# Down projections of a two-block kernel: T sums made ahead by POOL and kept in DRAM, bank sums added to the residual by accumulating DMAs

## The chip, the core and the metric

The kernel runs on one core of a Trainium2 chip. Its engines are TensorE (PE; its weight loads are listed as PEld), VectorE (DVE), ScalarE (ACT), GpSimd (POOL) and SyncE (SP), which here only issues DMAs. The metric is the device time of one execution in microseconds; less is better.

## The reference

Two blocks follow one another on `x`, 1024 tokens of 1024 features, in float32. Each is a mixer and then a gated feed-forward (FFN). The change touches the FFNs alone:

```python
# block 1                                             D_FF = 2816 = 22 x 128
gate, up = jnp.split(xn @ w_gate_up[l], 2, axis=-1)
x = x + (jax.nn.silu(gate) * up) @ w_down[l]
# block 2
u = causal_dwconv(h @ w_ffn_up[l], w_ffn_conv[l])
gate, val = jnp.split(u, 2, axis=-1)
x = x + (jax.nn.silu(gate) * val) @ w_ffn_down[l]
return rmsnorm(x, w_norm_final)
```

The mixer of block 2 runs between the two FFNs.

## The kernel before

**Products.** Every float32 operand is split into a high part (`wh`, `ah`, a copy on ACT, L256) and a low part (the difference, on DVE, L257), and a product is three matmuls of 128x512: high by high, high by low, low by high.

**Gate/up units.** Of the 22 feature tiles of an FFN, the first is made in `start`, the other 21 by `unit(f)`. A unit computes its gate and up tiles by the Strassen-Winograd scheme: seven products of 12 matmuls, 84 in all, into PSUM banks `st`. Its two weight tiles of 512 KB (up, then gate) come in through the ring `Weights`: SP issues the load (L129) into one of two raw buffers `wr` as soon as a raw buffer is free, so one unit's weights load while the unit before it runs. The sums S1 to S4 of the weights are made in place in the raw tile (L878): S3 and S4 on DVE, S1 and S2 on POOL (table `SE`). DVE adds the banks to `u` tiles (L980); the finished tile of hidden activations is stored to DRAM, `hd`, by SP (L1059, in `flush`).

**Down phase.** `strassen` multiplies hidden tiles 0 to 19 with the down weights, again by seven products (`DOWN`: A11 B11, A12 B21, S3 T3, A22 T4, S1 T1, S2 T2, S4 B22), each of 10 k-steps of 12 matmuls into four banks `dn`. The A side is split step by step into a ring `ah` of three tiles, the S sums of the hidden tiles are made in place (L1194; table `DE`: S1 and S2 on DVE, S3 and S4 on POOL). The B side: B11, B12 and B21 are loaded into home tiles and stay there, B22 comes through the weight ring, and T1 to T4 are made in place when the product T3 is split (L845: T3 and T1 on DVE, T2 and T4 on POOL). When a product ends, DVE adds each of its four banks to one to four places of the residual `x` (L980, `x<-dn,x`; places in `DOWN_SUMS`, 16 adds for A11, 56 per FFN), two after each k-step (`PB`), behind the splits that are queued before them. Hidden tiles 20 and 21 (`down`, matmuls `dn<-wh,hh`) come after five products in FFN1 and after all seven in FFN2.

Each engine takes its instructions in order; that order comes from a scheduler, by program order and priorities, not from a hand-written list.

Of the kernel before, what the change touches and what calls it, by code (L numbers as in the profile page):

```python
# [8 lines left out]
F32 = mybir.dt.float32  # L9
# [34 lines left out]
SE, TE, ME = dict(S3=vec_, S1=pool_, S2=pool_, S4=vec_), dict(T1=vec_, T2=pool_, T3=pool_, T4=pool_), vec_  # L44
# [8 lines left out]
DE = dict(S3=pool_, T3=vec_, T1=vec_, T2=pool_, T4=pool_, S1=vec_, S2=vec_, S4=pool_)  # L53
# [14 lines left out]
DOWN = (("A11", "B11"), ("A12", "B21"), ("S3", "T3"), ("A22", "T4"), ("S1", "T1"), ("S2", "T2"), ("S4", "B22"))  # L68
DOWN_SUMS = dict(A11=((0, 0), (0, 1), (1, 0), (1, 1)), A12=((0, 0),), S3=((1, 0), (1, 1)), A22=((1, 0),),
# [88 lines left out]
class Kern:  # L158
# [6 lines left out]
    def setup(self):  # L165
# [5 lines left out]
        self.hd = self.dram.tile([NF, P, S], F32, name="hd")  # L171
        self.ident = c.tile([P, P], F32, name="ident")
# [643 lines left out]
    def plan_ffn(self, which):  # L816
# [5 lines left out]
        for f in range(1, NF):  # L822
            units[f] = self.add_unit(*[up[:, :, o + f * P:o + (f + 1) * P] for o in (0, DFF)])
# [15 lines left out]
    def add_down(self, home, name, k, dn):  # L839

        W, nc = self.W, self.nc
        raw = W.load([(0, dn[:, ND + k:ND + k + 2, 512:])], 2, 512) if name in ("T3", "B22") else None

        def tt(out, in0, in1, what):
            DE[what](nc).tensor_tensor(out=out, in0=in0, in1=in1, op=ALU.subtract)  # L845

        def make(hi, lo):
            out = []
            for j in range(2):
                h, l = (v[:, j * 512:(j + 1) * 512] for v in (hi, lo))  # L850
                b11, b12, b21 = (home.get((q, k + j)) for q in ("B11", "B12", "B21"))
                b22 = None if raw is None else W.raw[raw][:, j * 512:(j + 1) * 512]
                if name == "T3":
                    src = home["T3", j]
                    tt(src, b22, b12, "T3")
                    tt(b12, b12, b11, "T1")
                    tt(b11, b22, b12, "T2")
                else:
                    src = dict(B11=b11, B21=b21, T4=b21, T1=b12, T2=b11, B22=b22)[name]
                    if name == "T4":  # L860
                        tt(b21, b21, b11, "T4")
                self.split(h, l, src)
                out.append((h, l))
            return out
        return W.slot(make, raw)

    def add_unit(self, gate, up):
# [9 lines left out]
        def tt(name, in0, in1, op, what):  # L877
            SE[what](nc).tensor_tensor(out=raw(name), in0=raw(in0), in1=raw(in1), op=op)  # L878
# [63 lines left out]
    def ffn(self, which):  # L942
# [118 lines left out]
        def unit(f):  # L1061
# [74 lines left out]
        def fetch(q, k0, k1):  # L1136

            f = k0 + ND * ((q[2] if q[0] == "A" else q[1]) == "2")
            c = 512 * ((q[1] if q[0] == "A" else q[2]) == "2")
            src = self.hd[f:f + k1 - k0, :, c:c + 512].rearrange("k p c -> p k c") if q[0] == "A" else \  # L1140
                dn[:, f:f + k1 - k0, c:c + 512]
            nc.sync.dma_start(out=places[q, k0][:, :k1 - k0, :], in_=src)
# [8 lines left out]
        def down_load():  # L1151

            for q, part in (("A11", "hi0"), ("B11", "lo0")):
                place(q, self.xnp.tile([P, KT, 512], F32, tag=part, name=q), 0, KT)
            for k in range(0, KT, 2):
                fetch("A11", k, k + 2)
                fetch("B11", k, k + 2)
# [3 lines left out]
        def down_open():  # L1161
# [4 lines left out]
            ring["ah"] = [d.tile([P, 2, 512], F32R, name=f"ah{i}") for i in range(AR)]  # L1166
            d = tc.alloc_tile_pool(name=f"dm{which}", bufs=1, reuse_waits="tile")
            dp.append(d)
            for j in range(2):
                home["T3", j] = d.tile([P, 512], F32, name=f"T3{j}")  # L1170
            ring["a22"] = [d.tile([P, 512], F32, name=f"a22{i}") for i in range(A2)]
            for q in ("A11", "B11", "A21", "B12"):
                place(q, d.tile([P, ND - KT, 512], F32, name=f"{q}x"), KT, ND)
            for q, part in (("A21", "hi1"), ("B12", "lo1")):
                place(q, self.xnp.tile([P, KT, 512], F32, tag=part, name=q), 0, KT)
            fetch("A11", KT, ND)
            fetch("B11", KT, ND)
            fetch("A12", 0, ND // 2)
            fetch("A12", ND // 2, ND)
            for i in range(AR):  # L1180
# [39 lines left out]
        def load_rest():  # L1220

            dp.pop().release()
# [8 lines left out]
        def strassen():  # L1231
            pool.release()
            last = None
            d2 = tc.alloc_tile_pool(name=f"dr{which}", bufs=1, side="right", reuse_waits="tile")
            dp.append(d2)
            self.psum(dn=(1, 8))
            place("B21", d2.tile([P, ND, 512], F32, name="B21"), 0, ND)
            for q in ("B21", "A21", "B12"):
                cuts = ((0, ND // 2), (ND // 2, ND)) if q == "B21" else ((0, KT // 2), (KT // 2, KT), (KT, ND))
                for k0, k1 in cuts:  # L1240
                    fetch(q, k0, k1)
            for k in range(A2):
                load22(k)
            sums = []
# [1013 lines left out]
```

## Time and profile before

| | before |
| --- | --- |
| median of 3 runs | 2538.17 us (2536.41 to 2547.12) |
| profiled execution | 2533.62 us, its span 2531.9 us |
| PE busy | 2420.6 us, 96% |
| DVE busy | 1856.3 us, 73% |
| ACT busy | 1145.8 us, 45% |
| POOL busy | 449.3 us, 18% |
| DMA | 196.58 MB, mean 78 GB/s |
| FFN1: starts of the units' matmuls; of the down phase's | 499.9 to 949.3 us; 949.5 to 1189.4 us |
| FFN2: starts of the down phase's matmuls | 2285.5 to 2524.2 us |

The profile's page gives shares over the whole span; stages differ in what limits them, so the rows below are taken from single stretches. A clock of 1.00 in a window is TensorE's full clock. A wait in the table of waits is time in which an engine stood still, put down to the instruction that released it. FFN1's down phase holds five products before tiles 20 and 21 and two after; FFN2's holds all seven.

### The profile page before, as it was taken

What the parts mean: (1) busy time and instruction counts of PE and PEld (TensorE: products, weight loads), DVE (VectorE), ACT (ScalarE), POOL (GpSimd) and SP (SyncE); (2) the same over time, 40 slices, a digit from 0 to 9 for tenths busy, and PEclk for the clock granted to TensorE, in tenths of its full rate; (3) what the DMA queues carried; (4) which work ended last, traced back from release to release, by engine and by line L of the source; (5) the groups of instructions that cost most, each with busy time, mean ns of one, the idle gap of its engine ahead of it and who ended that gap; (6) DMA issues with size and microseconds to landing.
All of it is one profiled execution on the core that took longest, in us unless ns stands there. A gap on an engine that the chain in (4) does not pass through costs nothing. (4 is left out here: it accounts for less than half of the span.)

```text
span 2531.9 us, 33317 instructions
## 1 busy us (share of the span) xinstructions
PE 2420.6 (96%) x12360; PEld 1993.5 (79%) x12360; DVE 1856.3 (73%) x3342; ACT 1145.8 (45%) x2290; POOL 449.3 (18%) x412
## 2 busy tenths in 40 slices
PE   7999999999999999899999999989899999999898
PEld 7977779978888887678877777879678888887677
DVE  5557788655555557977777868777878788878977
ACT  5356675342232233337432434776744434434243
POOL 1000002031111114500210111332341111113600
PEclk9999999999999999899999999999999999999999
DMA  4110002112223236213211112131212222227202
GB/s 152 51 34 21 22 26 92 42 48 78 75 83 91 76 110 240 75 42 123 62 42 50 30 46 64 40 137 49 75 51 84 92 75 75 84 93 265 67 33 109
DMA packets 194675, 196.58 MB, mean 78 GB/s; under 512 B 11613, under 2 KB 154032, under 8 KB 194512
## 3 DMA queue, kind: packets, MB, share of 16 engines
q1 hardware_dynamic: 189760, 178.74, 22.2%
q0 software_dynamic: 4752, 15.71, 1.8%
q8 instruction: 97, 1.59, 0.3%
q14 instruction: 66, 0.54, 0.1%
HBM read 155.76 MB, written 38.67 MB: 77 GB/s over the span
## 5 line engine op out<-in xcount | busy, mean ns | idle before, releaser
L257 DVE TENSOR_TENSOR wl<-wr,wh 128x512 fp32r<-128x512 f32 (+4 forms) x388 | 300.9, 805 | 320.1 <-ACT wh L256 316.2
L256 ACT CAST wh<-wr 128x512 fp32r<-128x512 f32 (+4 forms) x388 | 257.2, 696 | 583.4 <-PE st L973 363.9
L269 PE MATMUL dn<-wh,ah 128*128 128x512 f32 x560 | 225.6, 403 | 21.6 <-DVE ah L257 21.6
L267 PE MATMUL dn<-wh,ah 128*128 128x512 f32 x560 | 226.0, 404 | 5.4 <-ACT ah L256 2.2
L268 PE MATMUL dn<-wl,ah 128*128 128x512 f32 x560 | 224.0, 400 | 0.0
L980 DVE TENSOR_TENSOR u<-st,u 128x512 f32<-128x512 f32 x260 | 168.0, 685 | 30.7 <-PE st L973 29.3
L878 POOL TENSOR_TENSOR wr<-wr 128x512 f32<-128x512 f32 x42 | 55.2, 1315 | 692.3 <-DVE wr L878 692.3
L269 PEld LDWEIGHTS dn<-wh,ah 128*128 128x128 f32 x560 | 107.3, 192 | 56.3 <-DVE ah L257 30.8
L973 PE MATMUL st<-f1hi,wl 128*128 128x512 f32 x368 | 147.2, 400 | 0.0
L973 PE MATMUL st<-f2hi,wl 128*128 128x512 f32 x368 | 147.1, 400 | 0.0
L973 PE MATMUL st<-f2lo,wh 128*128 128x512 f32 x368 | 147.0, 400 | 0.0
L973 PE MATMUL st<-f1lo,wh 128*128 128x512 f32 x368 | 146.6, 398 | 0.0
L973 PE MATMUL st<-f1hi,wh 128*128 128x512 f32 x368 | 145.2, 394 | 0.7 <-ACT f1hi L256 0.7
L973 PE MATMUL st<-f2hi,wh 128*128 128x512 f32 x368 | 145.0, 394 | 0.7 <-ACT f2hi L256 0.7
L267 PEld LDWEIGHTS dn<-wh,ah 128*128 128x128 f32 x560 | 107.4, 192 | 32.8 <-ACT ah L256 4.1
L268 PEld LDWEIGHTS dn<-wl,ah 128*128 128x128 f32 x560 | 107.5, 192 | 24.0
L256 ACT CAST ah<-A 128x512 fp32r<-128x512 f32 x104 | 63.7, 619 | 109.7 <-PE dn L268 94.7
L257 DVE TENSOR_TENSOR ah<-A,ah 128x512 fp32r<-128x512 f32 x104 | 82.4, 796 | 41.9 <-ACT ah L256 38.9
L973 PEld LDWEIGHTS st<-f2hi,wh 128*128 128x128 f32 x368 | 70.4, 191 | 17.3 <-ACT f2hi L256 0.9
L973 PEld LDWEIGHTS st<-f1hi,wh 128*128 128x128 f32 x368 | 70.4, 191 | 17.2 <-ACT f1hi L256 0.9
L973 PEld LDWEIGHTS st<-f2lo,wh 128*128 128x128 f32 x368 | 69.6, 189 | 16.0
L973 PEld LDWEIGHTS st<-f1lo,wh 128*128 128x128 f32 x368 | 69.4, 189 | 16.1
(547 smaller groups left out, 7079.8 us busy)
## 6 DMA issues: line engine op xcount, KB each, us to landing
wr<-in_w_gate_up_dram SPq DMA_DIRECT2D x44, 512.0 KB, 4.3
hd<-sg SPq DMA_DIRECT2D x44, 512.0 KB, 3.2
wr<-in_w_ffn_up_dram SPq DMA_DIRECT2D x44, 512.0 KB, 3.9
wr<-in_w_mix_in_dram SPq DMA_DIRECT2D x28, 512.0 KB, 4.0
wr<-in_w_in_dram SPq DMA_DIRECT2D x16, 512.0 KB, 3.9
wr<-in_w_down_dram SPq DMA_DIRECT2D x12, 512.0 KB, 3.3
wr<-in_w_ffn_down_dram SPq DMA_DIRECT2D x12, 512.0 KB, 3.3
A<-hd SPq DMA_DIRECT2D x4, 1280.0 KB, 14.3
```

Of the source, the lines that this page charges most:

```text
L256: self.nc.scalar.copy(hi, src)
L257: self.nc.vector.tensor_tensor(out=lo, in0=src, in1=hi.bitcast(F32), op=ALU.subtract)
L267: mm(out, a[0], b[0], start=start, stop=False)
L268: mm(out, a[0], b[1], start=False, stop=False)
L269: mm(out, a[1], b[0], start=False, stop=stop)
L878: SE[what](nc).tensor_tensor(out=raw(name), in0=raw(in0), in1=raw(in1), op=op)
L973: mm(ps, a[p][:, kk, :], b[q][:, kk, :], start=start and kk == 0 and j == 0, stop=kk == n - 1 and j == 2, skip_group_check=True)
L980: nc.vector.tensor_tensor(out=out, in0=ps, in1=t, op=ALU.add)
```

## The change

1. **Early sums.** A generator, `prepare_down`, is stepped three times in each unit of FFN1. For both FFNs and each k-step it loads B12, B22, B11 and B21 (256 KB each, SP) into `pb` tiles, of which there are six; POOL makes T3, T1, T2 and T4 in place (L865) and issues a DMA for each to DRAM tensors `td` (L866). That is 80 loads, 80 sums, 80 stores.
2. **B side.** `add_down` loads every B operand, a home block or a T sum from `td`, through the weight ring, two k-steps (512 KB) at a time, split at once. The home tiles of B11, B12 and B21 and the sums in the down phase go.
3. **Residual.** For A11, A12, S3, A22 and S1 (`FAR`), ACT copies each bank to a `far` tile (four of them) and POOL issues a DMA that adds it to `x`, one for each place: 40 per FFN. S2 and S4 keep DVE's adds, 16 per FFN.
4. **Tables.** In FFN1's units S1 and S2 move from POOL to DVE. In the down phase S2 moves from DVE to POOL. The ring `ah` gets a fourth tile once the units' pool is released.

```diff
+FAR = ("A11", "A12", "S3", "A22", "S1")
-SE, TE, ME = dict(S3=vec_, S1=pool_, S2=pool_, S4=vec_), ...
+SE = {1: dict(S3=vec_, S1=vec_, S2=vec_, S4=vec_), 2: dict(S3=vec_, S1=pool_, S2=pool_, S4=vec_)}
-DE = dict(S3=pool_, T3=vec_, T1=vec_, T2=pool_, T4=pool_, S1=vec_, S2=vec_, S4=pool_)
+DE = dict(S3=pool_, S1=vec_, S2=pool_, S4=pool_)
-ND, AR, A2, PB = 10, 3, 2, 2
+ND, AR, AR0, A2, PB = 10, 4, 3, 2, 2
+    def add_down(self, which, name, k, dn):
+        f, c = k + ND * (name[1] == "2"), 512 * (name[2:] == "2")
+        return self.W.add([(0, dn[:, f:f + 2, c:c + 512] if name[0] == "B" else self.td[which, name][:, k:k + 2, :])],
+                          2, 512)
+    def prepare_down(self, pool):
+        nc = self.nc
+        for which in (1, 2):
+            dn = self.ffn_plan[which][3]
+            for k in range(ND):
+                def load(name):
+                    f, c = k + ND * (name[1] == "2"), 512 * (name[2] == "2")
+                    t = pool.tile([P, 512], F32, tag="pb", name="pb", bufs=6)
+                    nc.sync.dma_start(out=t, in_=dn[:, f, c:c + 512])
+                    return t
+                def keep(name, out, in0, in1, op):
+                    nc.gpsimd.tensor_tensor(out=out, in0=in0, in1=in1, op=op)
+                    nc.gpsimd.dma_start(out=self.td[which, name][:, k, :], in_=out)
+                b12, b22, b11, b21 = (load(n) for n in ("B12", "B22", "B11", "B21"))
+                yield
+                keep("T3", b22, b22, b12, ALU.subtract)
+                keep("T1", b12, b12, b11, ALU.subtract)
+                yield
+                keep("T2", b11, b11, b22, ALU.add)
+                keep("T4", b21, b21, b11, ALU.subtract)
+                yield
...
+        prep = self.prepare_down(pool) if which == 1 else iter(())
...
-                if k == ND - 1:
+                if k == ND - 1 and name in FAR:
+                    for t in range(4):
+                        u = d.tile([P, 512], F32, tag="far", name="far", bufs=4)
+                        nc.scalar.copy(u, banks[t])
+                        for c, e in DOWN_SUMS[name]:
+                            nc.gpsimd.dma_start(out=x[:, 4 * c + t, e * 512:(e + 1) * 512], in_=u, accum_op=ALU.add)
+                elif k == ND - 1:
```

How the change moves instructions, in the order in which each engine takes them. SP in FFN1's units, first before (`hd` is a unit's store, `wr` a weight load; wr_5970 and wr_6053 are unit 2's, wr_6118 and wr_6159 unit 3's, the next two unit 4's):

```order
L1059 DMA hd<-sg 128x1024
L129 DMA wr_5970<-in_w_gate_up_dram 128x8x128
L129 DMA wr_6053<-in_w_gate_up_dram 128x8x128
L129 DMA wr_6118<-in_w_gate_up_dram 128x8x128
L1059 DMA hd<-sg 128x1024
L129 DMA wr_6159<-in_w_gate_up_dram 128x8x128
L1059 DMA hd<-sg 128x1024
L129 DMA wr_6254<-in_w_gate_up_dram 128x8x128
L129 DMA wr_6295<-in_w_gate_up_dram 128x8x128
```

And after (wr_5978 and wr_6069 are unit 2's, wr_6138 and wr_6183 unit 3's):

```order
L861 DMA pb<-in_w_down_dram 128x512 x11
L1069 DMA hd<-sg 128x1024
L132 DMA wr_5978<-in_w_gate_up_dram 128x8x128
L861 DMA pb<-in_w_down_dram 128x512 x4
L132 DMA wr_6069<-in_w_gate_up_dram 128x8x128
L861 DMA pb<-in_w_down_dram 128x512 x10
L132 DMA wr_6138<-in_w_gate_up_dram 128x8x128
L861 DMA pb<-in_w_down_dram 128x512
L1069 DMA hd<-sg 128x1024
L132 DMA wr_6183<-in_w_gate_up_dram 128x8x128
L861 DMA pb<-in_w_down_dram 128x512 x11
```

The `pb` loads stand in bunches between the weight loads, twelve per unit as the list goes on; the last of the 80 stands ahead of unit 8's weights.

POOL in FFN1's units, after, from its first `pb` sum on, with what each instruction waits for (DMASW semaphores are those of its own DMAs, DMAHW those of SP's):

```order
L865 TENSOR_TENSOR pb_6023<-pb_6023,pb_6021 128x512 [waits DMAHW2_49,DMAHW1_49,Activation_49]
L866 DMA td1T3_69<-pb_6023 128x512 [waits DMASW5_49,Pool_49]
L865 TENSOR_TENSOR pb_6021<-pb_6021,pb_6025 128x512 [waits DMAHW3_49,PE_49]
L866 DMA td1T1_67<-pb_6021 128x512 [waits DMASW6_49,Pool_49]
L865 TENSOR_TENSOR pb_6025<-pb_6025,pb_6023 128x512
L865 TENSOR_TENSOR pb_6193<-pb_6193,pb_6191 128x512 [waits DMAHW6_49,DMAHW5_49]
L866 DMA td1T2_68<-pb_6025 128x512 [waits DMASW7_49,Pool_49]
L865 TENSOR_TENSOR pb_6027<-pb_6027,pb_6025 128x512 [waits DMAHW4_49]
```

Before, POOL had S1 and S2 of each unit in this place, two sums per unit; after, it has nothing but this chain until the last of the 80 stores.

ACT at the end of the product A11 in FFN1, after (`ah` are the A side's splits, `wh` the ring's):

```order
L262 CAST ah0_9174<-A12_9173 128x512
L1281 COPY far_9394<-dn_9216 128x512
L262 CAST hh21_10043<-raw_10041 128x1024
L1281 COPY far_9400<-dn_9217 128x512
L262 CAST ah1_9175<-A12_9173 128x512
L262 CAST wh121_9385<-wr79_9318 128x1024
L1281 COPY far_9406<-dn_9218 128x512
L1281 COPY far_9412<-dn_9219 128x512
```

DVE in the same place before, where the adds and the T sums stand between the splits:

```order
L980 TENSOR_TENSOR x_4781<-dn_8904,x_4781 128x512 x2
L845 TENSOR_TENSOR T30_8857<-wr72_8702,B12_8866 128x512
L845 TENSOR_TENSOR T31_8858<-wr72_8702,B12_8866 128x512
L257 TENSOR_TENSOR ah1_8852<-A12_8850,ah1_8852 128x512
L257 TENSOR_TENSOR wl123_9153<-B21_8891,wh123_9152 128x512 x2
L845 TENSOR_TENSOR B12_8866<-B12_8866,B11_8777 128x512
L257 TENSOR_TENSOR ah2_8853<-A12_8850,ah2_8853 128x512
```

The adds and T sums of the second list have left DVE; four bank copies have come to ACT.

## Rows read from the trace of the kernel before

**Rows 1.** Windows: gate/up units, FFN1's down phase, end of FFN2's; columns in its head.

```profile
core 0: us, PE busy (x) PEld busy (x) DVE busy (x) ACT busy (x) POOL busy (x), PEclk, DMA share, GB/s
545.00:928.00 383.00, 382.96 (x1651) 311.18 (x1650) 209.85 (x333) 110.14 (x195) 51.70 (x40) 1.00 0.27 81
949.00:1110.00 161.00, 148.21 (x604) 115.39 (x603) 139.27 (x181) 60.03 (x103) 69.52 (x42) 0.96 0.40 141
...
2420.00:2502.00 82.00, 82.00 (x355) 66.36 (x354) 54.88 (x86) 32.58 (x55) 0.60 (x1) 1.00 0.14 45
```

**Rows 2.** Matmuls into `dn`, FFN1 then FFN2: durations in ns, first and last start.

```profile
L267 PE MATMUL dn<-wh,ah x280: 387/397/628, 949.5 to 1189.0; 128*128 128x512 f32 x140
...
L267 PE MATMUL dn<-wh,hh x32: 388/394/395, 1110.1 to 1131.5; 128*128 128x512 f32 x32
...
L267 PE MATMUL dn<-wh,ah x280: 387/397/628, 2285.5 to 2501.6; 128*128 128x512 f32 x140
...
L267 PE MATMUL dn<-wh,hh x32: 388/394/395, 2502.3 to 2523.7; 128*128 128x512 f32 x32
```

**Rows 3.** PE's waits, 925 to 1300, then 2265 to 2532: total us, times, longest.

```profile
PE dn L269 <- DVE ah L257: 10.9, 8, 2.8
...
PE dn L269 <- DVE ah L257: 10.7, 8, 2.9
...
PE dn L267 <- DVE u L980: 1.6, 1, 1.6
```

**Rows 4.** Windows: one slice of FFN1's down phase, columns as in rows 1.

```profile
1015.00:1021.00 6.00, 4.33 (x10) 3.47 (x11) 6.00 (x5) 1.63 (x3) 4.69 (x4) 0.56 0.30 91
```

**Rows 5.** Groups by form, 949 to 1110: busy us, mean ns, idle before.

```profile
L257 DVE TENSOR_TENSOR ah<-A,ah 128x512 fp32r<-128x512 f32 x36 | 30.1, 844 | 9.9 <-ACT ah L256 9.8
...
L1194 POOL TENSOR_TENSOR A<-A,A 128x512 f32<-128x512 f32 x16 | 23.9, 1511 | 67.9 <-DVE ah L257 43.2 <-DVE A L1194 20.2 <-DVE x L980 4.5
...
L980 DVE TENSOR_TENSOR x<-dn,x 128x512 f32<-128x512 f32 x32 | 20.7, 678 | 0.0
...
L845 POOL TENSOR_TENSOR B<-wr,B 128x512 f32<-128x512 f32 x8 | 18.1, 2261 | 11.6 <-DVE B L845 9.7 <-ACT ah L256 1.9
...
L845 DVE TENSOR_TENSOR T<-wr,B 128x512 f32<-128x512 f32 x8 | 8.1, 1044 | 2.3 <-DMA wr<-in_w_down_dram 2.3
```

**Rows 6.** Groups by form, whole span: ACT, then DVE.

```profile
L256 ACT CAST wh<-wr 128x1024 fp32r<-128x1024 f32 x60 | 62.8, 1046 | 112.6 <-PE wo L269 40.7 <-PE gk L268 28.7 <-PE qkv L268 14.7
...
L1072 ACT COPY u<-st 128x512 f32<-128x512 f32 x42 | 24.7, 587 | 44.3 <-PE st L973 44.3
...
L257 DVE TENSOR_TENSOR wl<-wr,wh 128x1024 fp32r<-128x1024 f32 x60 | 76.7, 1282 | 86.0 <-ACT wh L256 83.9 <-PE vt L566 1.9
```

**Rows 7.** Line L1870, POOL's DMA issues of 256 KB: min/median/max, ns and us.

```profile
L1870 POOL DMA_DIRECT2D sqd<-sqt x8: 547/564/592, 1289.8 to 1563.1; - x8
...
DMA to landing us min/median/max: 2.4/2.9/5.6
```

**Rows 8.** Groups by form in the gate/up units, 545 to 928: DVE, then POOL.

```profile
L257 DVE TENSOR_TENSOR wl<-wr,wh 128x512 fp32r<-128x512 f32 x137 | 90.0, 692 | 162.0 <-ACT wh L256 161.3
...
L878 POOL TENSOR_TENSOR wr<-wr 128x512 f32<-128x512 f32 x20 | 25.8, 1291 | 345.8 <-DVE wr L878 345.8
```

**Rows 9.** DMA issues: number, KB each, median us from issue to landing.

```profile
wr<-in_w_gate_up_dram SPq DMA_DIRECT2D x44, 512.0 KB, 4.3
...
a<-hd SPq DMA_DIRECT2D x20, 256.0 KB, 2.7
```

**Rows 10.** Timelines of POOL, SP and ACT: start, us, instruction, count, idle before.

```profile
525.33 2.63 POOL L926 TENSOR_TENSOR xs<-xs 128x512 f32<-128x512 f32 x2 [0.33 <-PE xT L921]
...
640.99 4.00 SPq L129 DMA_DIRECT2D wr<-in_w_gate_up_dram  x2
...
629.31 1.14 ACT L256 CAST wh<-wr 128x512 fp32r<-128x512 f32 x2 [5.00 <-PE st L973]
...
640.64 0.59 ACT L1072 COPY u<-st 128x512 f32<-128x512 f32 x1 [1.32 <-PE st L973]
```

More of the change, by code (lines that the diff above doesn't have):

```diff
@@ L822, in plan_ffn @@
         for f in range(1, NF):
-            units[f] = self.add_unit(*[up[:, :, o + f * P:o + (f + 1) * P] for o in (0, DFF)])
+            units[f] = self.add_unit(which, *[up[:, :, o + f * P:o + (f + 1) * P] for o in (0, DFF)])
         home, slots = {}, {}
@@ L837, in plan_ffn @@
         self.ffn_plan[which] = (units, home, slots, dn, dw)
[L839 to L865, printed above, removed]
@@ L869, in add_unit @@
+    def add_unit(self, which, gate, up):
         W, nc = self.W, self.nc
@@ L877, in tt @@
         def tt(name, in0, in1, op, what):
-            SE[what](nc).tensor_tensor(out=raw(name), in0=raw(in0), in1=raw(in1), op=op)
+            SE[which][what](nc).tensor_tensor(out=raw(name), in0=raw(in0), in1=raw(in1), op=op)
         def cut(hi, lo, *names):
@@ L1093, in third @@
                 product(b1, A12, "B21", False)
+            next(prep, None)
             if f < NF - 1:
                 second()
+                next(prep, None)
                 third()
@@ L1114, in unit @@
             add(u2[:, main], b5, u2[:, main])
+            next(prep, None)
             if f == NF - 1:
@@ L1151, in down_load @@
         def down_load():
-            for q, part in (("A11", "hi0"), ("B11", "lo0")):
-                place(q, self.xnp.tile([P, KT, 512], F32, tag=part, name=q), 0, KT)
+            place("A11", self.xnp.tile([P, KT, 512], F32, tag="hi0", name="A11"), 0, KT)
             for k in range(0, KT, 2):
                 fetch("A11", k, k + 2)
-                fetch("B11", k, k + 2)
         ring = {}
@@ L1165, in down_open @@
             place("A12", d.tile([P, ND, 512], F32, name="A12"), 0, ND)
[L1166 removed]
+            ring["ah"] = [d.tile([P, 2, 512], F32R, name=f"ah{i}") for i in range(AR0)]
             d = tc.alloc_tile_pool(name=f"dm{which}", bufs=1, reuse_waits="tile")
             dp.append(d)
[L1169 to L1170 removed]
             ring["a22"] = [d.tile([P, 512], F32, name=f"a22{i}") for i in range(A2)]
[L1172 removed]
+            for q in ("A11", "A21"):
                 place(q, d.tile([P, ND - KT, 512], F32, name=f"{q}x"), KT, ND)
[L1174 to L1175 removed]
+            place("A21", self.xnp.tile([P, KT, 512], F32, tag="hi1", name="A21"), 0, KT)
             fetch("A11", KT, ND)
[L1177 removed]
             fetch("A12", 0, ND // 2)
             fetch("A12", ND // 2, ND)
[L1180 removed]
+            for i in range(AR0):
                 operand(i)
@@ L1233, in strassen @@
             last = None
-            d2 = tc.alloc_tile_pool(name=f"dr{which}", bufs=1, side="right", reuse_waits="tile")
-            dp.append(d2)
+            d = tc.alloc_tile_pool(name=f"dr{which}", bufs=1, side="right", reuse_waits="tile")
+            dp.append(d)
+            ring["ah"] += [d.tile([P, 2, 512], F32R, name=f"ah{i}") for i in range(AR0, AR)]
             self.psum(dn=(1, 8))
[L1237 to L1241, printed above, removed]
+            for k0, k1 in ((0, KT // 2), (KT // 2, KT), (KT, ND)):
+                fetch("A21", k0, k1)
             for k in range(A2):
                 load22(k)
+            for i in range(AR0, AR):
+                operand(i)
             sums = []
@@ L1282, in strassen @@
                 W.done(slots[DOWN[-1][1], ND - 2])
+                dp.pop(1).release()
             return last
@@ L1300, in ffn @@
             down(range(2 * ND, NF), self.tail2())
-            dp[1].release()
+            for d in dp[:0:-1]:
+                d.release()
     def tail1(self):
```

16 lines of the change are left out of this document (7 added, 9 removed).

## The prediction

> **What bounds the kernel now.** I read the page and the windows first: PE is busy nearly everywhere, so time can only be won where it waits or runs at a lowered clock, and lost where something new makes it wait. In the gate/up units of the first FFN the reader is to see PE busy 382.96 of 383 us at full clock, with DVE busy 209.85, POOL 51.70 and the DMA engines 0.27 [rows 1]: PE is the bound, all else has room. In the down phase of the first FFN (949 to 1110) PE is busy 148.21 of 161 at a clock of 0.96, and DVE 139.27 [rows 1]. The starts of the `dn` matmuls give the length of both phases [rows 2]. From the first `wh,ah` to the first `wh,hh` matmul it is 1110.1 - 949.5 = 160.6 us in FFN1, for five products of 120 matmuls, and 2502.3 - 2285.5 = 216.8 us in FFN2, for seven. A matmul at full clock costs 82.00 / 355 = 0.231 us [rows 1], so the phases need 600 x 0.231 = 138.6 and 840 x 0.231 = 194.0. Lost are 22.0 and 22.8 us, 44.8 together. The table of PE's waits names who ended them: 10.9 us on DVE's `ah` lows in FFN1, 10.7 in FFN2, each in eight waits of up to 2.9 us [rows 3]. The rest is clock: where PE had waited, slices show a granted clock of 0.56, near the lower level (1.2 of 2.4 GHz), with DVE busy 6.00 of 6.00 us [rows 4]. So DVE bounds these stretches.
>
> **The change, part one: less DVE work in the down phases (gain).** Of 56 adds of a bank to `x` in each FFN, 40 leave DVE. In FFN1's phase the row has 32 such adds, 20.7 us [rows 5]. The T sums go too; the largest DVE group alone is 8.1 us [rows 5]. That is 28.8 of DVE's 139.27, over twice what PE waited for it. B operands now come through the weight ring for all products, split two steps at a time; that split shows 1.046 us on ACT and 1.282 on DVE [rows 6]. DVE's load per two steps (24 matmuls, 5.54 us) becomes 1.282 + 2 x 0.844 for two `ah` lows [rows 5] = 3.0. ACT's is 1.046 + 2 x 0.587 (a copy of 128x512 [rows 6]) plus four copies of a bank in five such pairs, again 0.587 each, 2.7. Both are half busy, so the copies are hidden, and they free the banks earlier than adds queued behind splits do. POOL takes 40 DMA issues per FFN, at 0.564 each [rows 7] 22.6 us, in place of its T sums (one group of them alone is 18.1 us in FFN1 [rows 5]), so little is added to it in sum. It also takes the S2 sums, so in the A22 product it does 20 sums at 1.511 [rows 5] and four issues, 32.5 us, beside 27.7 us of matmuls. The S2 and S4 sums are needed only later, but the S2 sum releases the two `a22` buffers: I price this between 0 and 5 us an FFN. One stall is not this overload and stays: 1.6 us on `u` at FFN2's start [rows 3]. The gain is 44.8 less some 2 of these and 2 to 3 of the A22 excess: **40 us**, from 32 to 43.
>
> **Part two: early sums in the units of FFN1 (loss).** For each of 2 x 10 k-steps POOL now does four sums and issues four stores, and SP issues four loads of 256 KB. None of this is PE's work. But SP takes its list in order, and the order above shows the loads ahead of the units' weights: 15 before unit 2's second weight (wr_6069), 26 before unit 3's (wr_6183), and 12 more for each unit up to unit 7, whose second weight stands behind 74; all 80 stand before unit 8. There are six `pb` buffers, so from the seventh on a load waits until the store of the sum six loads earlier has landed. Behind that waiting load stand the next weight and the next `hd` store; ACT and DVE wait for the weight to split it, and PE for the splits. So the units of FFN1 may go no faster than POOL's chain: three k-steps per unit.
>
> The chain's period P per k-step is not in the trace and has to be bounded. POOL's time: 4 x 1.291 (a `wr` sum beside a half-busy DVE [rows 8]) + 4 x 0.564 (a store's issue [rows 7]) = 7.4 us is the floor. With sums of 1.511, as POOL's took in the down phase, it is 8.3; with 2.261, the dearest there, it is 11.3 [rows 5]. The round of one buffer is a second limit: sum 1.5, issue 0.57, landing 2.9 [rows 7], load 2.7 [rows 9] = 7.7. The two are near one another, so not every buffer wait hides behind POOL's work, and 24 x 256 KB, 6 MB, more travel per unit than before. I take **P = 8.9**: 8.3 plus 0.6 for such waits (an allowance between 0 and the 2.7 by which the longest landing, 5.6, exceeds the median [rows 7]). Moving S1 and S2 of these units from POOL to DVE I cost at nothing: 2 x 0.69 us [rows 8] more per unit of 19.5, on an engine busy 55% there; its cover would be gone only where DVE's adds are already late, which the 3 us below take in.
>
> When does unit 7's second weight land? Now it is the second of the two issues that start at 640.99 and end 4.00 later, at about 644.6 [rows 10], and lands 4.3 later [rows 9]: 648.9. After: POOL is free of earlier work at 528 (525.33 + 2.63 [rows 10]), the first load takes 2.7, so the chain starts at about 531. The 74th load needs 17 k-steps' stores: 531 + 17 x 8.9 = 682.3; the last store lands 2.9 later, the weight 4.3 later: 689.5. That is 40.6 late. At present such a weight comes early: unit 6's second is split from 629.31 on, as soon as it lands, and unit 6's first product (12 matmuls, 2.8 us) ends with the copy of its bank at 640.64 [rows 10], so the unit starts at 637.8 and the slack is 8.5. After, that slack doesn't count: DVE's queue has the next unit's split and S sums ahead of the present unit's adds, so a late weight holds the last product of the present unit too. From landing to the next unit's start there are then a split on ACT (0.6), some seven DVE operations of 0.69 [rows 8] and 2.8 of matmuls, 8.2 in sum; 11 where the matmuls run at half clock after the wait, 13.6 where DVE also waits out two of POOL's sums. So 0 to 5 us, and 3 taken, come on top: **loss 44 us**, in general 531 + 17P + 7.2 - 648.9 + 3 = 17P - 107.7. After unit 8 the loads are gone, and what is late stays late, since PE has no idle time there to make it up.
>
> What a page would add: the Trainium skill (SBUF — State Buffer, section "Who interferes with whom") states that a DVE operation with two SBUF inputs and a GpSimd operation that reads SBUF hold a shared port in turn, the later one blocked until the first ends. The trace agrees in part: 1.291 us a sum where DVE is half busy, 2.261 where it is busy 87% [rows 1, 5, 8]. Read strictly, with 2.261 throughout, the loss would be 17 x 11.3 - 107.7 = 84 us; the sum goes without it.
>
> **The sum.** 44 lost, 40 gained: +4 on the profiled run of 2533.62 us (span 2531.9), 2537.6. The median of the runs shown lies 4.5 above that run, so the forecast is **2542 us**. It is a difference of two large terms, and the sign hangs on P: both are equal at 17P = 147.7, P = 8.7. About 0.5%, 12.7 us, is what a measurement can tell from no change: P below 7.9 makes it faster by that, P above 9.4 slower.
>
> **Rivals.**
> 1. The chain runs at POOL's floor, P = 7.4: loss 18, net -22, 2516. For it: POOL does nothing else there, and the six buffers hold one and a half k-steps. Against: every one of 74 loads would have to come in time through one ordered queue.
> 2. POOL's sums stretch beside DVE, in the units of FFN1: P = 10.1, midway between 8.9 and 11.3; loss 64, net +24, **slower**, 2562. It decides from P = 9.4, a sum of about 1.65 us with the same allowance. For it: DVE gets S1 and S2, and works in bunches. Against: the `wr` sums at 1.291 beside the same DVE. The page named above speaks for it too.
> 3. The change doesn't hold the weights at all (loads and stores hide, SP never waits long): net -40, 2498. Against: 3 x 7.4 = 22.3 us of POOL per unit already exceeds 19.5; it would need the chain to run well ahead of the units before unit 2.
> 4. Accumulating DMAs are slow. The trace has none. If they went one after the other, at 2.9 each as a plain store lands, 40 make 116 us, within FFN1's 138.6; at 5.6 they make 224, beyond it. From 138.6 / 40 = 3.5 us each they hold the four `far` buffers, ACT's copies and the banks. At about 4 us FFN1's gain of 20 is gone: net +24, 2562.
>
> **How the numbers follow.** The forecast (P from 7.9 to 9.4) has 0.46, nearly all of it within 0.5%, rival 1 0.14, rival 2 0.22, rival 3 0.08, rival 4 0.10. Faster is rivals 1 and 3: 0.22. Slower is 2 and 4 and a little of the forecast: 0.34. The rest, 0.44, is within. The range leaves out rival 3 and the far ends of P: from 2513, just below rival 1, to 2567, just above rivals 2 and 4.
>
> **What would show it.** In the trace of after: SP's `pb` loads waiting, `hd` stores 25 to 28 us apart instead of 19.5 from about 560 to 700 and 19.5 again from unit 8 on; PE idle there on the splits of late weights; POOL's sums at 1.5 us, eight POOL instructions per 8.9 us. In the down phases: 141 and 197 us from first `wh,ah` to first `wh,hh`, no long wait on DVE's `ah`, DVE near half busy, full clock. Wrong would be: units that keep 19.5 us (rival 3), sums near 2 us (rival 2), PE waiting in the down phases for ACT's copies or `far` buffers (rival 4).

## The result and the profile after

The kernel became slower: 2610.03 us (median of 4 runs, 2606.68 to 2613.88) against 2537.47 (the three runs in the table of before and one more), ratio 1.0274 with a 95% interval of 1.0254 to 1.0294. The forecast was 2542, the range ended at 2567. The first lines of the page of after, to be read beside the table of before:

```profile
span 2605.0 us, 33769 instructions
...
PE 2431.8 (93%) x12360; PEld 2005.6 (77%) x12360; DVE 1878.2 (72%) x3174; ACT 1158.5 (44%) x2260; POOL 579.0 (22%) x590
```

The starts of the `dn` matmuls in FFN1 and FFN2 (as rows 2) say where the time went:

```profile
L273 PE MATMUL dn<-wh,ah x280: 388/395/628, 1037.9 to 1266.6; 128*128 128x512 f32 x140
...
L273 PE MATMUL dn<-wh,hh x32: 392/397/398, 1187.7 to 1209.3; 128*128 128x512 f32 x32
...
L273 PE MATMUL dn<-wh,ah x280: 388/395/628, 2364.4 to 2574.4; 128*128 128x512 f32 x140
...
L273 PE MATMUL dn<-wh,hh x32: 392/397/398, 2575.1 to 2596.7; 128*128 128x512 f32 x32
```

| stretch | before | after | difference |
| --- | --- | --- | --- |
| start to FFN1's first `wh,ah` | 949.5 | 1037.9 | +88.4 |
| FFN1, first `wh,ah` to first `wh,hh` | 160.6 | 149.8 | -10.8 |
| from there to FFN2's first `wh,ah` | 1175.4 | 1176.7 | +1.3 |
| FFN2, first `wh,ah` to first `wh,hh` | 216.8 | 210.7 | -6.1 |
| rest of the span | 29.6 | 29.9 | +0.3 |

The sum is +73.1, the difference of the two spans. Both terms of the forecast have the right sign and the wrong size: the loss is 88 instead of 44, the gain 17 instead of 40.

Windows of after, columns as in rows 1: most of the time of the early sums, the units that follow them, and FFN1's down phase.

```profile
545.00:760.00 215.00, 144.33 (x564) 114.78 (x563) 151.62 (x128) 36.52 (x65) 139.78 (x151) 0.82 0.71 234
760.00:1037.00 277.00, 275.14 (x1186) 223.44 (x1184) 169.61 (x267) 81.90 (x144) 0.00 (x0) 1.00 0.29 92
...
1037.00:1188.00 151.00, 145.35 (x602) 115.65 (x603) 103.96 (x91) 66.57 (x98) 80.96 (x65) 0.97 0.76 209
```

While the early sums run, PE is busy 144 of 215 us at a clock of 0.82; after them it is full again (275.14 of 277 us) and nothing is made up. In the down phase DVE has fallen as forecast, from 139.27 of 161 [rows 1] to 103.96 of 151 us.

**One unit, before and after.** The timelines show what PE waits for. SP in after, around the `hd` store that ends a unit, then SP in before at such a store:

```profile
651.44 0.38 SPq L132 DMA_DIRECT2D wr<-in_w_gate_up_dram  x1
652.01 0.43 SPq L1069 DMA_DIRECT2D hd<-sg  x1
652.53 0.41 SPq L861 DMA_DIRECT2D pb<-in_w_ffn_down_dram  x1
653.04 1.50 SPq L132 DMA_DIRECT2D wr<-in_w_gate_up_dram  x1
```

```profile
640.35 0.34 SPq L1059 DMA_DIRECT2D hd<-sg  x1
```

In after, the `hd` store one unit earlier had gone out at 619.52, so this unit took 32.5 us instead of 19.5. But the second weight goes out 1.0 us after the `hd` store; in before it went out some 4.3 us after it, as the second of the two issues that start at 640.99 [rows 10]. It is not late in SP's list. What SP waited for in after, from 560 to 760:

```profile
SPq L132 <- DVE wr L888: 60.1, 7, 15.0
SPq L861 <- DMA td1T<-pb: 42.4, 20, 6.4
SPq L861 <- DMA td2T<-pb: 41.1, 15, 7.4
```

At the early loads (L861) SP does wait for stores to land, 83.5 us in 35 waits. But when it comes to the weights behind them (L132), it waits once more, for DVE, 60.1 us in seven waits, because DVE has not yet freed the raw buffer. So it is not the chain that the weights wait for last: the chain waits for the units. Then ACT, DVE and PE of after in the next unit, from the landing of that weight on:

```profile
660.26 1.14 ACT L262 CAST wh<-wr 128x512 fp32r<-128x512 f32 x2 [8.15 <-DMA wr<-in_w_gate_up_dram]
```

```profile
660.91 2.36 DVE L263 TENSOR_TENSOR wl<-wr,wh 128x512 fp32r<-128x512 f32 x2 [8.08 <-ACT wh L262]
663.19 2.23 DVE L888 TENSOR_TENSOR wr<-wr,wr 128x512 f32<-128x512 f32 x1
665.46 3.31 DVE L888 TENSOR_TENSOR wr<-wr 128x512 f32<-128x512 f32 x1
668.69 0.68 DVE L990 TENSOR_TENSOR u<-st,u 128x512 f32<-128x512 f32 x1
669.29 1.81 DVE L888 TENSOR_TENSOR wr<-wr,wr 128x512 f32<-128x512 f32 x1
671.02 1.87 DVE L990 TENSOR_TENSOR u<-st,u 128x512 f32<-128x512 f32 x3
```

```profile
671.84 0.77 PE L983 MATMUL st<-f1hi,wh 128*128 128x512 f32 x1 [11.29 <-DVE u L990]
```

In after PE has five such waits for DVE's adds from 500 to 800 us, and one of 12.5 us for a split on ACT:

```profile
PE st L983 <- DVE u L990: 58.2, 5, 14.7
```

DVE of before in the same place:

```profile
629.96 1.29 DVE L257 TENSOR_TENSOR wl<-wr,wh 128x512 fp32r<-128x512 f32 x2 [4.92 <-ACT wh L256]
631.17 0.68 DVE L878 TENSOR_TENSOR wr<-wr,wr 128x512 f32<-128x512 f32 x1
632.27 3.21 DVE L980 TENSOR_TENSOR u<-st,u 128x512 f32<-128x512 f32 x5 [0.41 <-PE st L973]
```

From the split of the late weight to the second add on the `u` tiles, which PE needs for the unit's last product, it is some 11 us in after (660.91 to 671.84) and 3.6 in before (629.96 to about 633.5). The two splits take 2.36 instead of 1.29, and the S sums 2.23, 3.31 and 1.81 instead of 0.68 for the one that DVE had. The adds, which read a bank in PSUM, keep 0.68. PE stands still for 11.29 us, and its first matmul after that takes 0.77: the clock granted from 671 to 674 us is 0.50, the lower of its two levels. POOL's sums stand beside all of it; two of its lines there:

```profile
663.59 1.27 POOL L865 TENSOR_TENSOR pb<-pb 128x512 f32<-128x512 f32 x1
...
665.72 2.48 POOL L865 TENSOR_TENSOR pb<-pb 128x512 f32<-128x512 f32 x2
```

DVE's sum of 663.19 ends 0.56 us after the first of these lines, its sum of 665.46 ends 0.57 us after the second. Groups by form, DVE in after from 545 to 760, then the same of before, then POOL of after:

```profile
L263 DVE TENSOR_TENSOR wl<-wr,wh 128x512 fp32r<-128x512 f32 x47 | 60.6, 1317 | 62.6 <-ACT wh L262 62.4
L888 DVE TENSOR_TENSOR wr<-wr,wr 128x512 f32<-128x512 f32 x21 | 38.3, 1826 | 0.0
...
L888 DVE TENSOR_TENSOR wr<-wr 128x512 f32<-128x512 f32 x7 | 18.3, 2611 | 0.2
```

```profile
L257 DVE TENSOR_TENSOR wl<-wr,wh 128x512 fp32r<-128x512 f32 x77 | 50.8, 695 | 89.3 <-ACT wh L256 88.8
...
L878 DVE TENSOR_TENSOR wr<-wr,wr 128x512 f32<-128x512 f32 x22 | 15.1, 686 | 0.0
```

```profile
L865 POOL TENSOR_TENSOR pb<-pb 128x512 f32<-128x512 f32 x75 | 98.7, 1320 | 38.4 <-DMA pb<-in_w_ffn_down_dram 22.3 <-DMA pb<-in_w_down_dram 15.1
```

POOL's sums are hardly stretched (1320 ns against 1291 [rows 8]); DVE's operations with two operands in SBUF are, from 695 to 1317 and from 686 to 1826 and 2611 ns. The Trainium skill (SBUF — State Buffer, section "Who interferes with whom") states that such an operation and a GpSimd operation that reads SBUF hold a shared port in turn and that the second to issue is blocked until the first ends. The trace agrees that one holds up the other, and shows who pays here: DVE, hardly POOL. That the first to issue wins it does not show: by the records' start times both DVE sums above began before the POOL sums that they outlasted.

### The profile page after: what moved, and what is told of

Same layout as the page of the kernel before. It is cut to its first block, busy times and chain, and to the rows that moved or that the text cites. A ratio compares the mean times of both kernels' runs of the same rounds, so it can differ in the third digit from the quotient of the medians.

```text
span 2605.0 us, 33769 instructions
## 1 busy us (share of the span) xinstructions
PE 2431.8 (93%) x12360; PEld 2005.6 (77%) x12360; DVE 1878.2 (72%) x3174; ACT 1158.5 (44%) x2260; POOL 579.0 (22%) x590
## 5 line engine op out<-in xcount | busy, mean ns | idle before, releaser
L263 DVE TENSOR_TENSOR wl<-wr,wh 128x512 fp32r<-128x512 f32 (+3 forms) x438 | 417.5, 977 | 354.0 <-ACT wh L262 348.4
L262 ACT CAST wh<-wr 128x512 fp32r<-128x512 f32 (+3 forms) x438 | 319.2, 755 | 728.5 <-PE st L983 399.2
L983 PE MATMUL st<-f1hi,wh 128*128 128x512 f32 x368 | 151.1, 411 | 70.7 <-DVE u L990 58.2
L983 PEld LDWEIGHTS st<-f1hi,wh 128*128 128x128 f32 x368 | 73.7, 201 | 89.9 <-issue 73.1
L1199 POOL TENSOR_TENSOR A<-A,A 128x512 f32<-128x512 f32 x32 | 62.3, 2397 | 352.1 <-PE dn L274 310.7
L263 DVE TENSOR_TENSOR ah<-A,ah 128x512 fp32r<-128x512 f32 x104 | 75.2, 736 | 61.0 <-ACT ah L262 60.9
L865 POOL TENSOR_TENSOR pb<-pb 128x512 f32<-128x512 f32 x80 | 105.4, 1323 | 45.3 <-DMA pb<-in_w_ffn_down_dram 22.3
L888 POOL TENSOR_TENSOR wr<-wr 128x512 f32<-128x512 f32 x21 | 27.2, 1293 | 346.4 <-DVE wr L888 346.4
L888 DVE TENSOR_TENSOR wr<-wr,wr 128x512 f32<-128x512 f32 x105 | 96.7, 921 | 0.1
```

The lines of the kernel that those rows point to most:

```text
L262: self.nc.scalar.copy(hi, src)
L263: self.nc.vector.tensor_tensor(out=lo, in0=src, in1=hi.bitcast(F32), op=ALU.subtract)
L865: nc.gpsimd.tensor_tensor(out=out, in0=in0, in1=in1, op=op)
L888: SE[which][what](nc).tensor_tensor(out=raw(name), in0=raw(in0), in1=raw(in1), op=op)
L983: mm(ps, a[p][:, kk, :], b[q][:, kk, :], start=start and kk == 0 and j == 0, stop=kk == n - 1 and j == 2, skip_group_check=True)
L1199: DE[what](nc).tensor_tensor(out=out, in0=in0, in1=in1, op=op)
```

## The experiments

Theories: A, weights stand in SP's list behind the chain (the prediction's); B, POOL's early sums hold DVE at a shared port; C, the added traffic makes late weights land later. Each kernel is after with the edit shown. The table gives the first `dn` matmul of FFN1 (before 949.5) and the usual distance of two `hd` stores while the early work runs (before 19.5).

| run | early loads and stores | early sums | first `dn` | unit | total |
| --- | --- | --- | --- | --- | --- |
| after | dense, in SP's list | dense | 1037.9 | 32 to 34 | 2610.03 |
| e1 | none | none | 952.6 | 19.5 | 2523.33 |
| e2 | 4 of each per unit | 4 per unit, at the late weight | 1058.7 | 22 to 26 | 2628.37 |
| e3 | none | dense | 991.0 | 27 to 28 | 2561.95 |
| e4 | dense, in SP's list | none | 1011.7 | 27 to 31 | 2581.16 |
| e5 | 4 of each per unit | none | 964.8 | 20 | 2530.66 |
| e6 | 4 of each per unit | 4 per unit, still beside the split | 1020.9 | 23 | 2592.98 |
| e9 | 4 of each per unit | 4 per unit, in DVE's gap | 956.6 | 19.7 | 2529.57 |
| e12 | dense, POOL's queue | dense | 1037.6 | 31 to 35 | 2608.0 |
| e13 | dense, POOL's queue | none | 993.5 | 25 to 28 | 2560.83 |

### e1: no early sums

```diff
-        prep = self.prepare_down(pool) if which == 1 else iter(())
+        prep = iter(())
```

with each T operand loaded from a block of the down weights.

> Leaves out all 80 early loads, sums and stores; a T operand is loaded from a block of the down weights instead, of the same size, so the down phases move the same bytes and do the same work. All theories of the loss in FFN1's units (A: SP's ordered list, B: POOL's sums holding DVE at a shared port, C: the extra DMA traffic) expect the units back at 19.5 us each and the down phase's first matmul near 950 instead of 1038. It measures what the down phases alone gain: 17 us by the trace of after, so about 2521; by the prediction's 40 it would be 2498.

Measured: 2523.33 us, ratio 0.9943 (0.9918 to 0.9967). The units are back, which puts 85.3 us on the early work (1037.9 - 952.6) and leaves 3.1. Of these, 2.8 are one wait of PE just before the first `dn` matmul. It stands in the trace of every run that has S1 and S2 of FFN1's units on DVE, after included, and in none that has them on POOL (before, e6, e9, e10, e11), so it goes with them. Losses are therefore counted from e1's 952.6, those of e6, e9 and e11 from before's 949.5. The down phases take 1102.7 - 952.6 = 150.1 and 2486.1 - 2278.3 = 207.8 us, 19.5 less than before: that is all that part one is worth.

### e2: the order of SP's list

```diff
-                    nc.sync.dma_start(out=t, in_=dn[:, f, c:c + 512])
+                    ins = nc.sync.dma_start(out=t, in_=dn[:, f, c:c + 512])
+                    self.tc.add_manual_dep(ins.ins, self.last_w.name, NOSYNC, reason="after the weights")
```

`last_w` is the weight load issued last.

> The same 80 loads, sums and stores, but each group of four loads is tied behind the weight load issued last before it in the program, so that SP's list has four of them per unit instead of twelve. Theory A (the loss is the order of SP's list: weights wait behind early loads that wait for POOL's stores) expects the units at 19.5 us and about 2521 to 2526. Theory B (POOL's sums slow DVE) expects the same 80 sums to cost what they cost, spread over 20 units: 2580 to 2610. Theory C (traffic) expects a part back, since 4 x 256 KB each way per unit are a third of before: around 2550.

Measured: 2628.37 us, ratio 1.0354 (1.0315 to 1.0393), slower than after. Theory A fails as it stood. POOL and DVE of e2 in one unit:

```profile
600.96 1.69 POOL L866 TENSOR_TENSOR pb<-pb 128x512 f32<-128x512 f32 x1 [16.60 <-DMA pb<-in_w_down_dram]
...
603.52 1.30 POOL L866 TENSOR_TENSOR pb<-pb 128x512 f32<-128x512 f32 x1
```

```profile
601.42 1.78 DVE L889 TENSOR_TENSOR wr<-wr,wr 128x512 f32<-128x512 f32 x1
603.24 2.15 DVE L889 TENSOR_TENSOR wr<-wr 128x512 f32<-128x512 f32 x1
```

The early loads go out right behind the late weight and land with it, so POOL's four sums meet DVE's S sums in every unit, in 20 units instead of six.

### e3 and e4: the sums alone, the transfers alone

e3 runs the 80 sums on six tiles that are loaded once. e4 removes the sums and keeps the rest:

```diff
                 def keep(name, out, in0, in1, op):
-                    nc.gpsimd.tensor_tensor(out=out, in0=in0, in1=in1, op=op)
                     nc.gpsimd.dma_start(out=self.td[which, name][:, k, :], in_=out)
```

> 80 POOL sums in FFN1's units on six tiles that are loaded once; no further early loads, no stores; T operands are loaded from a block of the down weights, so results differ. Theory A and theory C expect no loss in the units (first matmul of the down phase near 950, about 2521). Theory B expects the loss to stay: first matmul near 1038, about 2610.

> The 80 loads and 80 stores in after's order, without the POOL sums between (unsummed blocks are stored, so results differ). Theory B expects the loss gone: about 2521. Theory C expects it to stay whole: about 2610, or more, since the transfers crowd closer. Theory A expects a part of it, since a load still waits for a store: four issues of 0.56 us, and a round of a buffer of 0.56 + 3.4 + 4.4 = 8.4 us for one and a half k-steps, make 5.6 us per k-step plus SP's own waits for weight buffers of 6.5 us per unit, 23 us per unit instead of 32.5: first matmul near 975, about 2545.

Measured (one run each): e3 2561.95 us, a loss in the units of 991.0 - 952.6 = 38.4; e4 2581.16, a loss of 59.1. Neither cause explains after's 85.3 alone, and their sum, 97.5, is more: they overlap. e3 has no transfer and no list, so its 38.4 are theory B by itself. In its first 135 us DVE's operations read:

```profile
L263 DVE TENSOR_TENSOR wl<-wr,wh 128x512 fp32r<-128x512 f32 x35 | 48.2, 1405 | 28.3 <-ACT wh L262 28.3
L883 DVE TENSOR_TENSOR wr<-wr,wr 128x512 f32<-128x512 f32 x16 | 20.8, 1297 | 0.0
```

In e4 DVE keeps 0.68 for each sum, and it is the weight that comes late. ACT and SP of e4:

```profile
630.54 1.14 ACT L262 CAST wh<-wr 128x512 fp32r<-128x512 f32 x2 [16.05 <-DMA wr<-in_w_gate_up_dram]
```

```profile
605.76 12.02 SPq L861 DMA_DIRECT2D pb<-in_w_ffn_down_dram  x9
...
619.69 0.66 SPq L132 DMA_DIRECT2D wr<-in_w_gate_up_dram  x1
```

Here theory A does act: without the sums the chain runs ahead, nine early loads hold SP's list from 605.76 on for 12.02 us, and the weights follow. And theory C: the weight issued at 619.69 is split from 630.54 on, 10.9 us later.

### e5 and e13: the transfers, spread and dense, without sums and without the list

e5 is e2 without the sums. e13 is e12 (below) without the sums.

> e2 without its 80 POOL sums: the loads, in groups of four behind each unit's weight, and the 80 stores stay (unsummed blocks are stored, so results differ). Theory B (in e2 it is the sums that hold DVE at a shared port, at the moment when DVE makes the late weights' sums) expects the units back at 19.5 us: first matmul of the down phase at 953 as in e1, about 2523. Theory C (the traffic itself) expects the 59 us that e4 lost against e1 to stay, as the bytes are the same: first matmul near 1012, about 2581. Theory A for e4's loss (bunches in SP's list) expects the same as B here.

> e12 without its POOL sums: 80 loads and 80 stores of 256 KB, all issued by POOL, as dense as POOL's issues and their landings allow (unsummed blocks are stored, so results differ). If e4's loss was SP's list, the units run at 19.5 to 20 us here: first matmul of the down phase at 953 to 960, about 2523. If it was the crowded traffic, which makes a late weight land later, a good part stays: first matmul at 980 to 1012, 2550 to 2580, and hd stores 24 us or more apart while the stores run.

Measured (one run each): e5 2530.66 us, a loss of 964.8 - 952.6 = 12.2 for the same bytes over 20 units, some 0.6 a unit; so in e2 the sums make 106.1 - 12.2 = 94, if the two simply add. e13 2560.83, a loss of 40.9 with no list and no sums. Landing times of the weight loads, 560 to 700 (minimum, median, maximum): first before, then after, then e13:

```profile
DMA to landing us min/median/max: 3.8/4.2/5.7
```

```profile
DMA to landing us min/median/max: 4.9/6.4/8.2
```

```profile
DMA to landing us min/median/max: 5.4/7.4/10.1
```

In that stretch before moves 80 GB/s, after 244, e13 299. So crowding alone costs 40.9 us in e13, and the list, by the difference of two single runs, about 18 more in e4 (59.1 - 40.9).

### e6 and e9: the same sums at another place in the unit

Both have e2's order and S1 and S2 on POOL. e6 ties the sums behind S2. e9 holds them back until DVE has finished the unit:

```diff
...
+                m = pool.tile([P, 1], F32, tag="mark", name="mark", bufs=2)
+                mark = nc.gpsimd.tensor_copy(m, self.last_sg[:, S - 1:S])
                 keep("T3", b22, b22, b12, ALU.subtract)
...
```

where `keep` ties each sum behind `mark`, `last_sg` is the tile of the unit's last multiply, and the generator's last step in a unit comes behind that multiply.

> e2 with two edits: the sums S1 and S2 of FFN1's units are on POOL again, as in the kernel before, and POOL's early sums are tied behind S2 of the unit, so that they run after the moment in which DVE and POOL prepare the next unit's operands. All 80 loads, sums and stores stay. If place decides (theory B with the place: only sums beside that moment cost PE time), the units take 19.5 to 20 us, first matmul near 955, about 2525. If each early sum costs DVE its time wherever it runs, the loss of e2 stays: first matmul near 1050, about 2620. In between, near 985 and 2555, if half of them still hit.

> All early loads, sums and stores of after, in e2's order of SP's list (four loads behind each unit's weights), but POOL's four sums of a k-step are held back by one unit: they start when DVE has finished the unit's last multiply, the moment of the hd store, where DVE next has one split to do in 8 us. S1 and S2 of FFN1's units are on POOL again, as in the kernel before. If the two causes found so far (weights behind the chain in SP's list; sums beside DVE's operations on the late weights) are all of the loss, the units come back: first matmul of the down phase at 950 to 965 (e5, traffic alone, 965), total 2520 to 2535. If an early sum costs PE time wherever it stands, the loss stays as in e6: near 1020, total 2593.

Measured: e6 2592.98 us, ratio 1.0195 (1.0176 to 1.0214); e9 2529.57, ratio 0.997 (0.9955 to 0.9986). In e6 the tie did not do what its expectation says: the tie left T3 and T1 of the next k-step ahead of the unit's S1 in POOL's list, and T2 and T4 then met the next splits. The pair of splits at that place took 5.08 us. In e9 POOL and DVE pass each other by:

```profile
643.59 0.58 POOL L874 COPY mark<-sg 128x1 f32<-128x1 f32 x1 [4.58 <-DVE sg L1059]
644.12 1.28 POOL L866 TENSOR_TENSOR pb<-pb 128x512 f32<-128x512 f32 x1
...
650.59 1.29 POOL L866 TENSOR_TENSOR pb<-pb 128x512 f32<-128x512 f32 x1
```

```profile
646.80 1.33 DVE L263 TENSOR_TENSOR wl<-wr,wh 128x512 fp32r<-128x512 f32 x1 [2.68 <-ACT wh L262]
654.04 1.29 DVE L263 TENSOR_TENSOR wl<-wr,wh 128x512 fp32r<-128x512 f32 x2 [5.91 <-ACT wh L262]
655.25 0.68 DVE L892 TENSOR_TENSOR wr<-wr,wr 128x512 f32<-128x512 f32 x1
```

The four sums run from 644.12 to 651.9, where DVE has one split (1.33 instead of 0.69, which nobody waits for). From the late weight's split at 654.04 on, no early sum stands beside DVE. All 80 loads, sums and stores are there, and the units lose 956.6 - 949.5 = 7.1 us in all instead of 85.3. e6 has as many of each at the same pace, only the sums' place differs, and loses 1020.9 - 949.5 = 71.4. So it is not the amount of early work but the place of the sums beside DVE that decides. For the transfers the density decides: 12.2 spread (e5) against 40.9 and 59.1 dense (e13, e4), single runs all three.

### e11 and e12: the edits of after undone one at a time

e11 puts S1 and S2 of FFN1's units back on POOL. e12 takes the early loads out of SP's list:

```diff
-                    nc.sync.dma_start(out=t, in_=dn[:, f, c:c + 512])
+                    nc.gpsimd.dma_start(out=t, in_=dn[:, f, c:c + 512])
```

> After with one edit undone: S1 and S2 of FFN1's units stay on POOL as before, and so stand in POOL's list among the early sums; SP's order of the early loads stays as in after. If the move of S1 and S2 to DVE was needed (POOL takes them late, behind sums that wait for loads), the loss grows: first matmul of the down phase beyond 1038, total above 2615. If the move is part of the loss (DVE has more operations beside POOL's sums in the tight moment), it shrinks by some 2 us a unit for seven units: near 1024, total near 2595.

> After with one edit: the 80 early loads are issued by POOL, not by SP, so no weight load stands behind them any more, and none of them behind a weight load; the sums still run as early and as densely as POOL can, with S1 and S2 on DVE. If the two causes add (weights in SP's list behind the chain, 59 us in e4; sums beside DVE, 38 us in e3), only the second is left: first matmul of the down phase at 985 to 1000, total 2558 to 2575. If SP's list was not a cause, the loss stays: near 1038, total 2610. If the sums do no harm without the list, 955 and 2523.

Measured: e11 2608.51 us, ratio 1.0282 (1.0258 to 1.0305), first `dn` at 1040.5, so who has S1 and S2 makes no difference to the total. e12 2608.0, ratio 1.0253 (1.0233 to 1.0273), first `dn` at 1037.6: with no weight behind an early load the loss is the same to 0.3 us. So the loss does not need SP's list; with dense sums and dense transfers, B and C suffice. That the two agree so closely is partly chance: in e12 the weights land later (a median of 7.9 us from 560 to 700, in after 6.4), and DVE's `wr<-wr,wr` sums are less stretched (1473 ns from 545 to 760, in after 1826). That the list held nothing in after rests on SP's waits there. The expectation that A and B add is refuted too.

### e7, e8 and e10: the down phases

e7 and e8 are e1 with one edit each, e10 is e9 with e7's:

```diff
 e7, e10
-DE = dict(S3=pool_, S1=vec_, S2=pool_, S4=pool_)
+DE = dict(S3=pool_, S1=vec_, S2=pool_, S4=vec_)
 e8
-FAR = ("A11", "A12", "S3", "A22", "S1")
+FAR = ()
```

> e1 (no early sums) with the S4 sums of the down phase on DVE instead of POOL. In after, POOL has S2 and S4 sums of 2.3 to 2.4 us beside a DVE that is always busy in the product A22, and PE loses about 8 us in each FFN there. If that is POOL falling behind with two sums a step, ten sums less on it give 10 to 16 us: about 2509 to 2513. If it is the sharing of a port, whoever has the sums, about 5 us or nothing: 2518 to 2523. If DVE becomes late instead, slower than e1: above 2528.

> e1 (no early sums) with all 56 adds to x per FFN on DVE again, in place of ACT's copies and POOL's accumulating DMAs; B operands still come through the weight ring. The prediction's reading (the adds on DVE are what held the ah lows, the DMAs are free) expects the gain to go: 2531 to 2539. The rival (with the T sums gone DVE has room for the adds, and the accumulating DMAs cost as much, since POOL's issues take 1.35 us each and DVE stands beside them) expects no loss or a gain: 2512 to 2524.

> e9 with the S4 sums of the down phase on DVE, as in e7. The first matmul of the down phase as in e9; the two down phases 149 and 204 us as in e7 instead of 150 and 208 as in e1, so 3 to 6 us less than e9. If e9's reading holds: 2515 to 2530.

Measured: e7 2519.34 us (ratio 0.9905, 0.9891 to 0.992), e8 2526.82 (0.9941, 0.9924 to 0.9957), e10 2524.74 (0.9948, 0.993 to 0.9967). The phases, FFN1 and FFN2: e1 150.1 and 207.8, e7 148.6 and 204.0, e8 150.1 and 205.7, e10 148.8 and 205.6. So the accumulating DMAs bring nothing that shows: with all 56 adds on DVE again the phases are as short. What helps is among what e8 keeps: the T sums out of the phase, B split two k-steps at a time, S2 on POOL, the fourth `ah` tile. No run takes these apart, and that it is the T sums is not shown. S4 on DVE is worth some 5 us in the phases of e7, and again from e9 (151.1 and 208.4) to e10; the totals of e1, e7 and e8 lie too near each other to tell more. e10, with all the work of the change, beats the kernel before by 0.5% and after by some 3%.

Where the rest of the gain went shows in the groups by form of after, 1037 to 1188:

```profile
L1199 POOL TENSOR_TENSOR A<-A,A 128x512 f32<-128x512 f32 x16 | 31.1, 2373 | 311.1 <-PE dn L274 310.7
...
L1199 DVE TENSOR_TENSOR A<-A,a 128x512 f32<-128x512 f32 x8 | 10.9, 1368 | 2.2 <-DMA a<-hd 2.2
```

POOL's sums take 2.373 us on average instead of the 1.511 of rows 5, but the mean is raised by overlapping records of five sums in a row from 1130.94 on; the others in the product A22 take 1.6 to 2.2. DVE's S1 sums take 1.368, and DVE is busy without a break from 1126 to 1138 and from 1144 to 1162: the same sharing as in the units. It isn't all, though. One DVE split takes 6.07 us from 1129.46 on, in part beside POOL's issue of eight accumulating DMAs (7.08 us from 1126.57 on). And PE's longest wait in A22, 1.97 us for a split on ACT, follows a wait of ACT of 9.32 us for a load of a hidden tile (`a<-hd`), while the DMA share was 0.95 to 1.08 (1126 to 1144). No run takes these shares apart.

## Why the prediction was wrong

- **"So the units of FFN1 may go no faster than POOL's chain": this step failed.** I read the order of SP's list as a wait of the weights for the chain. In after the second weight goes out 1.0 us after the `hd` store, earlier than in before, and SP waits for DVE at the weights; e12 has no such list and loses the same. In place of that wait the runs show DVE held up beside POOL's sums (38.4 us alone in e3, gone with the place in e9) and weights that land late in dense traffic (40.9 alone in e13). The chain's period came out at 10.3 us per k-step (from the first sum at 534.9 to the end of the last near 741, over 20) instead of 8.9, but it followed the units rather than leading them. The buffers were no second limit near POOL's 7.4 either: a round of 7.7 us serves six loads, one and a half k-steps, so it allows 5.1 per k-step. Only e4 shows the list at work, at some 18 us, once the sums are gone.
- **"So 0 to 5 us, and 3 taken, come on top": the right place, counted once instead of once a unit.** The section from the late weight's split to the unit's last product was in the sum, with seven DVE operations of 0.69. They took 0.68 to 3.31, some 11 us in all, and this returned in each of the six units that had early sums beside them, with PE's restart at the lower clock after it. The queue order in which a late weight holds the unit's last product was right.
- **Rival 2 had the mechanism and the wrong victim.** It let POOL's sums stretch beside DVE, and decided from sums of 1.65 us. They stayed at 1.32; DVE's operations went to two and three times their length. The sentence that the prediction gives from the Trainium skill (SBUF — State Buffer, "Who interferes with whom") has both engines wait for the port; I took the rows of POOL alone for the price. That the strict reading there, 2.261 throughout, gives 84 us, next to the 85.3 measured, is luck: POOL's sums did not take 2.261, and the units did not wait for the chain.
- **The traffic was an allowance of 0.6 us in P.** It was a cause of its own: landings of 6.4 instead of 4.2 us, and 40.9 us alone in e13.
- **The gain: 17 instead of 40 (19.5 in e1).** "Both are half busy, so the copies are hidden" held for ACT (66.57 of 151 us); DVE stayed busy for 103.96, 69%. PE's long waits on DVE's `ah` are gone (1.6 us in FFN1, 4.2 in FFN2 instead of 10.9 and 10.7). What stays, 11 us in FFN1 and 17 in FFN2 of the 44.8, are waits of up to 2.8 us at the start and in the product A22, with the lowered clock after them. I had priced A22 at 0 to 5 us an FFN, with POOL's sums at 1.511 and four issues at 0.564; there were eight issues, 7.08 us. The adds were credited with a gain that e8 shows they don't have; that DVE has room for them without the T sums is my reading of it.
- Rival 4 (accumulating DMAs hold the phase) did not come: each lands after 9.0 us, but several are under way at once. Rivals 1 and 3 fell with the units.

What stays open: how after's 85.3 us divide between sums and crowding. Alone they cost 38.4 and 40.9, each at another density than in after, and both lengthen the same section. In the unit shown the late weight comes no later behind the `hd` store: ACT splits it 8.25 us after (652.01 to 660.26), in before 8.45 us after (620.86 to 629.31 [rows 10]).

## What to carry to other kernels

Work on an idle engine is not free when it reads SBUF beside a tight section of another engine: find the few microseconds of each iteration in which PE's next product hangs on DVE, and place the new work outside them (e9: the same work, 7 us instead of 85). A delay found in a repeated section is a price per iteration, not once. And before blaming a queue's order, look at what the queue itself waits for: here SP waited for DVE.

## What the runs showed of the hardware

- Beside POOL's 128x512 sums, in after from 545 to 760, DVE's operations with two SBUF operands went from 0.69 us to 1.3 (splits) and to 1.8 and 2.6 (sums) on average, its adds from PSUM stayed at 0.68, and POOL's sums stayed at 1.32. In e3, where POOL's sums follow one another without issues between them, POOL paid too: 1.56 to 1.70 a sum.
- An accumulating DMA of 256 KB into SBUF occupied POOL 1.35 us for its issue and landed after 9.0; a plain store of 256 KB to DRAM took 0.55 and 3.4. The line of after for the first:

```profile
L1283 POOL DMA_DIRECT2D x<-far x80: 851/1348/3372, 1070.6 to 2522.5; - x80
...
DMA to landing us min/median/max: 3.4/9.0/15.1
```

- A weight load of 512 KB landed after 4.2 us where the core moved 80 GB/s and after 7.4 where it moved 299 (e13), medians both.
